# A fifth hidden tile by quarters in the second half of an FFN's output product

## The chip, the cores and the metric

The kernel runs on one core of a Trainium2 chip. The metric is the device time of one execution in microseconds (us). Each engine works through its own instructions in the order in which they were written into its queue: TensorE (PE; PEld is its loading of the stationary operand), VectorE (DVE), ScalarE (ACT), GpSimd (POOL), and SyncE (SP), which here issues the DMA transfers. Engines wait for one another by semaphores.

## The reference

One decoder layer on 512 tokens of width 1024: a first SwiGLU FFN, a token mixer, a second FFN, each between a norm before and a norm after, added to the residual stream.

```python
def swiglu_ffn(x, w_in, w_out):
    gate, up = jnp.split(x @ w_in, 2, axis=-1)
    return (jax.nn.silu(gate) * up) @ w_out

x = x + 0.5 * rms_norm(swiglu_ffn(rms_norm(x, norm_pre[l, 0]), ffn1_w_in[l], ffn1_w_out[l]),
                       norm_post[l, 0])
mixed = token_mixer(rms_norm(x, norm_pre[l, 1]), ...)
x = x + rms_norm(mixed, norm_post[l, 1])
x = x + 0.5 * rms_norm(swiglu_ffn(rms_norm(x, norm_pre[l, 2]), ffn2_w_in[l], ffn2_w_out[l]),
                       norm_post[l, 2])
```

The hidden width is 2816. The change lies in the product of the hidden values (512 x 2816) with `w_out` (2816 x 1024), which occurs twice, once in each FFN. The text calls the two FFNs the two layers.

## The kernel before

**Numbers in two parts.** TensorE multiplies in a rounded 32-bit format. To keep the precision, each operand is split into a high part (a cast on ScalarE) and a low part (the value less the high part, a subtraction on VectorE), and each product is made of three matmuls: high by high, high by low, low by high. A "split" below is such a pair of cast and subtraction. Every weight tile (L273 and L275 in `split`) and every hidden tile (`two_parts`, L812 and L813) is split once per use, 1024 columns wide on 128 partitions.

**The output product.** `ffn_out` (L858) works on the 1024 output columns in two halves. In each half it goes through 11 hidden tiles of 256 hidden columns, numbered 0 to 10, in the order `OUT` gives, and adds the products up in PSUM. The four blocks of 128 tokens and two quarters of the columns (256 each) are held in four accumulators `C[u][v]`: u is 0 for the even token blocks (0 and 2) and 1 for the odd ones. C takes four of the eight PSUM banks.

**Plain and quartered tiles.** A plain tile (`plain`, L886) takes 48 matmuls of 256 columns. A tile in `QUARTERED` is done by Strassen's method in Winograd's form: its hidden values and its weight are each cut into four quarters, sums of quarters are formed, and 7 products of 6 matmuls do the work of 8, 42 in all (`quartered`, L906, and `product`, L898). Four of the 7 products go into accumulators of their own, `M` (the other four PSUM banks), shared by all quartered tiles of a half; three go straight into C. After the last quartered tile of a half `common` (L922) copies one of the M to SBUF (ScalarE) and forms three more sums from M (four operations of VectorE, L863), and `add` (L932) adds the results to C, two operations for the odd blocks and two for the even ones (L863 as well: it is the line of the helper). The additions to the odd blocks need the copy and the second of the four operations, those to the even blocks the last two.

**What a quartered tile costs elsewhere.** Its weight is split twice: the three quarters used as they are (768 columns wide), then, after `sum_quarters` (L303, four VectorE operations of 256 columns, L306) has put the sums in the raw tile's place, all 1024 columns. Its hidden values need the parts of three quarters (`h_quarters`, L822), the sums (`h_sums`, L837, operations L844) and the parts of the sums (`s_tile`, L851). A tile that is quartered in both halves keeps the parts of its quarters and its sums (`stay`: the sums overwrite the hidden values) and makes only the parts of the sums anew in the second half.

**Places.** Split weights lie in four slots (`WBUF`): while one is multiplied, up to three are made ready, and a slot is free once TensorE has used its tile. Split hidden tiles and sums lie in three "s" places. The parts of quarters lie in the four idle places of the normed input (`PLACES`, `x_place`) or, for tiles 3 and 7, in the idle raw buffers of the weight loads (`RAW`, three of them; the name "once" in the profile). `LATER` puts hidden tiles 0 and 7 of the second half into those input places once the parts there are used. Tiles 9 and 10 keep their split form from the first half to the second. The "gpre" place holds a row of norm gains, and is read only while an input is normed.

**The end of the second half.** The last four tiles of `OUT[1]` (`LAST`) are plain and are taken together: for each token block i all four tiles are multiplied (`chunk`, L984; 48 matmuls per block, 12 per tile), so that the blocks are finished one after another and the norm after the FFN (`last`, L504) can begin. For block 0 the tiles go strictly one after the other. The odd additions (L982) stand ahead of the blocks, the even ones (L994) behind block 0. W0, W5, W7 and so on are the weights of hidden tiles 0, 5, 7.

**What sets the order.** The program is written as straight Python; a planner then fixes the order of each engine's instructions by a list of priorities (the order of writing) and its own estimate of when operands and places are free. So an instruction written later can stand ahead of an earlier one whose operand is not expected yet. On the chip this order is fixed. Loads of weights are issued on SP as soon as their raw buffer comes free in this plan.

Of the kernel before, what the change touches and what calls it, by code (L numbers as in the profile page):

```python
# [9 lines left out]
F32R = mybir.dt.float32r  # L10
AF = mybir.ActivationFunctionType
ALU = mybir.AluOpType
PSUM = bass.MemoryType.PSUM

P = 128
T = 512
D = 1024
# [5 lines left out]
RAW, WBUF, PAD, LATE, NEXT, FRONT, STEP = 3, 4, 128, 112, 64, 96, 16  # L23
PAIRS = NF // 2
# [54 lines left out]

QUARTERED = [(2, 3, 4, 6, 7, 8), (2, 4, 6, 8)]
OUT = [list(range(PAIRS)), [9, 2, 4, 10, 6, 8, 0, 1, 3, 5, 7]]
LAST = 4
PLACES, LATER = {2: 1, 4: 2, 6: 0, 8: 3}, {0: (1, 0), 7: (2, 3)}

AGAIN, ROWS = (9, 10), (18, 19, 20, 21)

# [27 lines left out]
class Layer:  # L116
# [705 lines left out]
    def h_quarters(self, k2, n=None):  # L822

        src = self.by_chunk(k2)
        parts = self.x_place(n) if n is not None else [
            self.wp.tile([P, D], F32R, tag="raw", bufs=RAW, name=self.nm("once"))[:, P - 2 * STEP :] for _ in range(2)
        ]
        parts = [v[:, : 3 * QUARTER].rearrange("p (k c t) -> p k c t", c=2, t=P) for v in parts]
        self.two_parts(*(v[:, 0] for v in parts), src[:, 0, 1])
        self.two_parts(*(v[:, 1:] for v in parts), src[:, 1])  # L830
        return [[None] + [v[:, j] for j in range(3)] for v in parts]
# [5 lines left out]
    def h_sums(self, k2, stay):  # L837

        a = self.by_chunk(k2)
        f = self.hf[:, 2 * k2 : 2 * k2 + 2, :]  # L840
        if not stay:
            f = self.sp.tile([P, 2, T], F32, tag="xn", bufs=1, name=self.nm("hsum"))
        v = f.rearrange("p k (c u t) -> p k u c t", u=2, t=P)
        tt = lambda out, x, y, op: self.nc.vector.tensor_tensor(out, x, y, op=op)  # L844
        tt(v[:, 0, 0], a[:, 0, 1], a[:, 0, 0], ALU.subtract)
        tt(v[:, 1, 0], v[:, 0, 0], a[:, 1, 0], ALU.add)
        for k in range(2):
            tt(v[:, k, 1], a[:, k, 1], v[:, 1, 0], ALU.subtract)
        return f

    def s_tile(self, f):  # L851
# [6 lines left out]
    def ffn_out(self, gpost_row, scale, after, trans, head):  # L858
# [10 lines left out]
        def more(n):  # L869
            while count[0] < min(n, len(seq)):  # L870
                half, k2 = seq[count[0]]
                count[0] += 1
                if k2 in QUARTERED[half]:
                    if k2 not in kept:
                        stay = k2 in QUARTERED[1]
                        kept[k2] = self.h_quarters(k2, PLACES.get(k2)), self.h_sums(k2, stay)
# [99 lines left out]
        for k2 in OUT[1][-LAST:]:  # L976
            ws.append(self.pull())
            more(n + 1)
            n += 1
        hs = [made.popleft()[0] for _ in range(LAST)]  # L980

# [836 lines left out]
```

## Time and profile before

| what | value |
|---|---|
| median of 3 runs | 937.53 us (937.38 to 937.99) |
| profiled execution, its own time | 939.23 us |
| its span | 937.5 us |
| granted TensorE clock | 0.999 |
| PE busy | 929.0 us (99%) |
| DVE busy | 772.9 us (82%) |
| ACT busy | 511.5 us (55%) |
| output product, layer 1 | from 223.99 to about 341.7 us |
| its second half, layer 1 | from about 282.5 us |

Times in rows count from the start of the span. In rows in order of time the columns are: start, length from the first start to the last end, engine, line, operation, output <- inputs with their shapes, and how many instructions are merged (x6); in brackets stands how long the engine was idle before it and what ended that. Operations of one engine overlap a little, so that the next starts before the last has ended. In rows of groups the columns are: what it is and how often, then busy time in us and the mean length of one in ns, then the idle time ahead of them.

### The profile page before, as it was taken

To read this page: it belongs to the slowest core of one execution; us is meant where nothing else is said; L and a number is where in the kernel's file an instruction comes from. 1 tells how busy PE (TensorE), PEld (TensorE's weight loads), DVE (VectorE), ACT (ScalarE), POOL (GpSimd) and SP (SyncE) were. 2 spreads that over 40 slices of the span, in tenths; PEclk is the share of its full clock that TensorE was granted. 3 is DMA by queue.
4 is the path that set the end of the run, shared out by engine and by line. 5 is a ranking of instruction groups with operands and counts; after the bars stand their busy time and mean duration, and the time that the engine had idled before them with its cause. 6 is when DMAs were issued, how large, how long until landed. Compare 5 with 4: busy or idle time off the path is not lost.

```text
span 937.5 us, 18056 instructions
## 1 busy us (share of the span) xinstructions
PE 929.0 (99%) x7471; PEld 894.4 (95%) x7471; DVE 772.9 (82%) x1044; ACT 511.5 (55%) x735; POOL 107.1 (11%) x172
## 2 busy tenths in 40 slices
PE   9999999999999999999999999999999999999997
PEld 7999999999999999998887887899999999999997
DVE  6899988889988876698846665799899889998884
ACT  7645455557456467956632445595354545655541
POOL 3530000000001045200011310314000000000101
PEclk9999999999999999999999999999999999999999
DMA  9252443332352034421312124352354435324212
GB/s 317 89 157 91 128 126 108 99 108 78 116 164 91 24 87 121 111 68 45 91 45 68 46 91 143 104 181 67 115 158 135 136 116 157 108 90 131 78 45 91
DMA packets 86956, 101.35 MB, mean 108 GB/s; under 512 B 4277, under 2 KB 66777, under 8 KB 86874
## 3 DMA queue, kind: packets, MB, share of 16 engines
q1 hardware_dynamic: 86586, 99.68, 34.8%
q8 instruction: 58, 0.95, 0.4%
q10 hardware_dynamic: 288, 0.52, 0.2%
q14 instruction: 24, 0.20, 0.1%
HBM read 98.10 MB, written 2.10 MB: 107 GB/s over the span
## 4 chain that ended last, share of the span: by engine, by line
PE 61%; ACT 1%; DMA 0%; DVE 0%; issue 0%; POOL 0%; DVEq 0%; POOLq 0%; ACTq 0%; SPq 0%
PE ps L603 22%; PE ps L893 7%; PE ps L533 6%; PE ps L901 5%; PE ps L179 5%; PE ps L181 4%; PE ps L180 4%; PE ps L1307 2%; PE ps L348 1%; PE ps L543 1%; PE ps L1482 0%; DMA raw<-in_ffn_w_in_dram 0%; PE ps L1393 0%; PE ps L1589 0%; PE ps L1562 0%; PE ps L1348 0%
## 5 line engine op out<-in xcount | busy, mean ns | idle before, releaser
L273 ACT CAST w<-raw 128x1024 fp32r<-128x1024 f32 (+1 forms) x238 | 244.4, 1034 | 233.1 <-PE ps L603 93.5
L275 DVE TENSOR_TENSOR w<-raw,w 128x1024 fp32r<-128x1024 f32 (+1 forms) x238 | 291.6, 1232 | 36.1 <-ACT w L273 35.3
L603 PE MATMUL ps<-xq,w 128*128 128x256 f32 x2016 | 237.4, 277 | 0.0
L603 PEld LDWEIGHTS ps<-xq,w 128*128 128x128 f32 x2016 | 233.2, 188 | 0.0
L603 PE MATMUL ps<-sq,w 128*128 128x256 f32 x1512 | 178.3, 277 | 0.3
L603 PEld LDWEIGHTS ps<-sq,w 128*128 128x128 f32 x1512 | 174.6, 188 | 0.9 <-ACT ps L654 0.9
L893 PE MATMUL ps<-w,hs 128*128 128x256 f32 x960 | 113.0, 276 | 0.0
L893 PEld LDWEIGHTS ps<-w,hs 128*128 128x128 f32 x960 | 110.7, 188 | 0.0
L289 DVE TENSOR_TENSOR raw<-raw,raw 128x1024 f32<-128x1024 f32 x72 | 89.9, 1251 | 8.1 <-DMA raw<-in_ffn_w_in_dram 6.6
L179 PE MATMUL ps<-w,xq 128*128 128x512 f32 x192 | 78.8, 411 | 0.1
L180 PE MATMUL ps<-w,xq 128*128 128x512 f32 x192 | 74.9, 391 | 0.1
L181 PE MATMUL ps<-w,xq 128*128 128x512 f32 x192 | 75.0, 392 | 0.0
L438 POOL TENSOR_SCALAR col<-col 128x1 f32<-128x1 f32 x24 | 9.0, 377 | 513.8 <-ACT junk L437 513.7
L533 PE MATMUL ps<-xq,w 128*128 128x256 f32 x480 | 58.1, 282 | 0.0
L901 PE MATMUL ps<-w,hs 128*128 128x256 f32 x480 | 57.7, 276 | 0.0
L533 PEld LDWEIGHTS ps<-xq,w 128*128 128x128 f32 x480 | 56.9, 189 | 0.5 <-issue 0.5
L901 PEld LDWEIGHTS ps<-w,hs 128*128 128x128 f32 x480 | 55.9, 188 | 0.0
L179 PEld LDWEIGHTS ps<-w,xq 128*128 128x128 f32 x192 | 36.1, 188 | 8.3 <-issue 0.9
L181 PEld LDWEIGHTS ps<-w,xq 128*128 128x128 f32 x192 | 36.0, 188 | 8.2 <-DVE xq L355 0.3
L812 ACT CAST hs<-hf 128x1024 fp32r<-128x1024 f32 x32 | 33.7, 1052 | 17.4 <-PE ps L901 10.7
L180 PEld LDWEIGHTS ps<-w,xq 128*128 128x128 f32 x192 | 36.2, 188 | 7.2 <-DVE w L281 0.5
L813 DVE TENSOR_TENSOR hs<-hf,hs 128x1024 fp32r<-128x1024 f32 x32 | 39.1, 1221 | 1.3 <-ACT hs L812 1.2
(258 smaller groups left out, 1140.4 us busy)
## 6 DMA issues: line engine op xcount, KB each, us to landing
raw<-in_ffn_w_in_dram SPq DMA_DIRECT2D x98, 512.0 KB, 3.7
raw<-in_ffn_w_out_dram SPq DMA_DIRECT2D x44, 512.0 KB, 4.2
raw<-in_w_mix_in_dram SPq DMA_DIRECT2D x28, 512.0 KB, 3.7
raw<-in_w_mix_out_dram SPq DMA_DIRECT2D x8, 512.0 KB, 3.9
out_dram<-xs SPq DMA_DIRECT2D x8, 256.0 KB, 2.0
xs<-in_x_dram SPq DMA_DIRECT2D x6, 256.0 KB, 4.1
gpost<-in_norm_post_dram SPq DMA_DIRECT2D x3, 512.0 KB, 3.5
gpre<-in_norm_pre_dram SPq DMA_DIRECT2D x2, 512.0 KB, 4.5
```

The source lines that it names most:

```text
L179: mm(ps, sh, mh, start=start, stop=False, **kw)
L180: mm(ps, sh, ml, start=False, stop=False, **kw)
L181: mm(ps, sl, mh, start=False, stop=stop, **kw)
L273: nc.scalar.copy(hi, raw)
L275: self.low = nc.vector.tensor_tensor(lo, raw, hi.bitcast(F32), op=ALU.subtract)
L289: (nc.vector if late else nc.gpsimd).tensor_tensor(o, o, c, op=ALU.add)
L533: mm(ps[:, u0:u1], w[:, a, k, :], self.xop(k, b, u0, u1), start=k + n + m == 0, stop=k == ND - 1 and n == 2, skip_group_check=True,)
L603: self.nc.tensor.matmul(ps[:, c], wb[b][:, k, v], left[d][:, k, :], start=first and a + n + k == 0, stop=n == 2 and k == KH - 1, skip_grou ...
L812: self.nc.scalar.copy(hi, src)
L813: self.nc.vector.tensor_tensor(lo, src, hi.bitcast(F32), op=ALU.subtract)
L893: mm(out, a[kk][:, i * P : (i + 1) * P], w[:, b, kk, QUARTER * v : QUARTER * (v + 1)], start=begin and c == kk == n == 0, stop=kk == 1 and ...
L901: mm(ps[:, QUARTER * c : QUARTER * (c + 1)], A[a][:, c], B[b], start=begin and c == n == 0, stop=n == 2, skip_group_check=True,)
```

## The change

In the second half of the columns tile 3 is quartered as well, so that the second half has five quartered tiles instead of four. The order of the second half becomes 9, 2, 4, 10, 3, 6, 8 and then the last four, 0, 1, 5, 7; before it was 9, 2, 4, 10, 6, 8, 0 and then 1, 3, 5, 7. There is no plain tile between the last quartered tile and the last four any more.

The parts of tile 3's quarters are kept from the first half to the second in the two raw buffers in which they were made, and its sums overwrite its hidden values. Tile 7, quartered only in the first half, puts its high parts into the third raw buffer and its low parts into the "gpre" place. Hidden tile 0 of the second half goes to an "s" place instead of the input places.

In `h_sums` the last two of four operations (256 columns each) become one of 512 columns, one operand of which is repeated over its two rows. This holds for every quartered tile.

```diff
-QUARTERED = [(2, 3, 4, 6, 7, 8), (2, 4, 6, 8)]
-OUT = [list(range(PAIRS)), [9, 2, 4, 10, 6, 8, 0, 1, 3, 5, 7]]
-LAST = 4
-PLACES, LATER = {2: 1, 4: 2, 6: 0, 8: 3}, {0: (1, 0), 7: (2, 3)}
+QUARTERED = [(2, 3, 4, 6, 7, 8), (2, 3, 4, 6, 8)]
+OUT = [list(range(PAIRS)), [9, 2, 4, 10, 3, 6, 8, 0, 1, 5, 7]]
+LAST, APART = 4, 7
+PLACES, LATER = {2: 1, 4: 2, 6: 0, 8: 3}, {7: (2, 3)}
...
     def h_quarters(self, k2, n=None):

         src = self.by_chunk(k2)
-        parts = self.x_place(n) if n is not None else [
-            self.wp.tile([P, D], F32R, tag="raw", bufs=RAW, name=self.nm("once"))[:, P - 2 * STEP :] for _ in range(2)
-        ]
+        once = lambda pool, tag, bufs, o: pool.tile([P, D], F32R, tag=tag, bufs=bufs, name=self.nm("once"))[:, o:]
+        if n is not None:
+            parts = self.x_place(n)
+        else:
+            places = [(self.wp, "raw", RAW, P - 2 * STEP), (self.cp, "gpre", 1, STEP // 2)]
+            parts = [once(*places[k2 == APART and m]) for m in range(2)]
...
         tt(v[:, 0, 0], a[:, 0, 1], a[:, 0, 0], ALU.subtract)
         tt(v[:, 1, 0], v[:, 0, 0], a[:, 1, 0], ALU.add)
-        for k in range(2):
-            tt(v[:, k, 1], a[:, k, 1], v[:, 1, 0], ALU.subtract)
+        tt(v[:, :, 1], a[:, :, 1], v[:, 1:2, 0].broadcast_to([P, 2, 2, P]), ALU.subtract)
         return f
```

## The prediction

> **What bounds the kernel now.** I read the page first: TensorE is busy nearly the whole span and holds most of the chain of work that ended last. Then the waits of TensorE: in 937 us it waits twice, once at the start. So TensorE sets the time. Matmuls taken out come back as time, unless something new makes TensorE wait.
>
> ```profile
> span 937.5 us, 18056 instructions
> PE 929.0 (99%) x7471; PEld 894.4 (95%) x7471; DVE 772.9 (82%) x1044; ACT 511.5 (55%) x735; POOL 107.1 (11%) x172
> PE ps L175 <- POOL ident masks.py:199: 1.5, 1, 1.5
> PE ps L603 <- ACT xq L368: 0.2, 1, 0.2
> ```
>
> Next the stretch that is changed, the second half of the columns. The busy time of each engine by stretch (length, then PE, PEld, DVE, ACT) shows the first layer's tiles 6 and 8, plain tile 0, and the first token block of the last four tiles; the last row is tile 0 in the second layer.
>
> ```profile
> 302.87:307.63 4.76, 4.76 (x44) 4.76 (x43) 3.53 (x5) 3.42 (x4) 0.00 (x0) 1.00 0.15 30
> 307.63:312.39 4.76, 4.76 (x44) 4.76 (x43) 4.76 (x5) 3.48 (x5) 0.00 (x0) 1.00 0.23 88
> 312.39:317.83 5.44, 5.44 (x50) 5.44 (x49) 5.44 (x8) 1.58 (x2) 0.00 (x0) 1.00 0.00 0
> 317.83:323.27 5.44, 5.44 (x50) 5.44 (x49) 3.34 (x5) 1.05 (x1) 0.00 (x0) 1.00 0.01 3
> 904.07:909.51 5.44, 5.44 (x50) 5.44 (x49) 5.44 (x8) 1.58 (x2) 0.00 (x0) 1.00 0.00 0
> ```
>
> TensorE is full in every row, but VectorE is full too from 307.63 to 317.83. A quartered tile lasts 4.76 us and a plain one 5.44. Both layers show the same stretch, 591.68 us apart. TensorE's own rows in order of time are plain tile 0 (48 matmuls in 5.44 us, 0.113 us each) and then the first token block, three tiles and the fourth:
>
> ```profile
> 312.39 5.60 PE L893 MATMUL ps<-w,xq 128*128 128x256 f32 x48
> 317.83 4.24 PE L893 MATMUL ps<-w,hs 128*128 128x256 f32 x36
> 321.91 1.52 PE L893 MATMUL ps<-w,xq 128*128 128x256 f32 x12
> ```
>
> What VectorE does beside it, also in order of time:
>
> ```profile
> 284.20 0.95 DVE L275 TENSOR_TENSOR w<-raw,w 128x768 fp32r<-128x768 f32 x1
> 285.06 2.38 DVE L475 TENSOR_TENSOR y<-ps,gpost 128x256 f32<-128x256 f32 x6
> ...
> 301.53 1.80 DVE L306 TENSOR_TENSOR raw<-raw 128x256 f32<-128x256 f32 x4
> 304.53 1.22 DVE L275 TENSOR_TENSOR w<-raw,w 128x1024 fp32r<-128x1024 f32 x1 [1.19 <-ACT w L273]
> 305.67 1.22 DVE L813 TENSOR_TENSOR hs<-hf,hs 128x1024 fp32r<-128x1024 f32 x1
> ...
> 312.48 0.68 DVE L863 TENSOR_TENSOR hf<-ps,hf 128x512 f32<-128x512 f32 x1
> 313.08 1.21 DVE L813 TENSOR_TENSOR xq<-hf,xq 128x1024 fp32r<-128x1024 f32 x1
> 314.22 0.68 DVE L863 TENSOR_TENSOR hf<-ps,hf 128x512 f32<-128x512 f32 x1
> 314.82 1.22 DVE L275 TENSOR_TENSOR w<-raw,w 128x1024 fp32r<-128x1024 f32 x1
> 315.95 0.68 DVE L863 TENSOR_TENSOR hf<-hf,ps 128x512 f32<-128x512 f32 x1
> 316.55 1.22 DVE L813 TENSOR_TENSOR hs<-hf,hs 128x1024 fp32r<-128x1024 f32 x1
> 317.69 0.68 DVE L863 TENSOR_TENSOR hf<-ps,hf 128x512 f32<-128x512 f32 x1
> 318.29 1.29 DVE L863 TENSOR_TENSOR ps<-ps,hf 128x512 f32<-128x512 f32 x2
> 319.48 1.22 DVE L275 TENSOR_TENSOR w<-raw,w 128x1024 fp32r<-128x1024 f32 x1
> 322.79 1.38 DVE L863 TENSOR_TENSOR ps<-ps,hf 128x512 f32<-128x512 f32 x2 [2.10 <-PE ps L893]
> ```
>
> From 304.53 to 320.62 there is no idle time. By start to start a 1024-wide operation takes 1.14 us (304.53 to 305.67), a 512-wide one 0.60 (312.48 to 313.08), the 768-wide split 0.86 (284.20 to 285.06). The four L863 to hf are the common sums. The pair at 318.29 adds two of them to the odd accumulators, and that at 322.79 the others to the even ones. The split at 319.48 is the last weight, W7.
>
> **The change part by part.** *Matmuls.* Tile 3 goes from 48 to 42 matmuls in each layer: 5.44 - 4.76 = 0.68 us, twice, so -1.36 us if nothing waits. This is all the change can save on TensorE.
>
> *Weight of tile 3.* Instead of one 1024-wide cast and subtraction it needs a 768-wide pair, four quarter sums and the 1024-wide pair. On VectorE that adds 0.86 + 1.80 = 2.66 us per layer, on ScalarE one 768-wide cast of 0.83 us, hidden since ScalarE is busy 3.4 to 3.5 of 4.76 us there. The hidden tile costs the same: it is split once in this half, from the sums instead of the values.
>
> ```profile
> L273 ACT CAST w<-raw 128x768 fp32r<-128x768 f32 x20 | 16.6, 831 | 0.2
> ```
>
> *The order.* Plain tile 0 moves behind the last quartered tile, into the last four, and tile 3 goes ahead of 6 and 8. So the four common sums and the splits for the last four tiles lose the 5.44 us of plain tile 0 as cover, and must run beside the last tiles themselves.
>
> *Where VectorE stands then.* After tile 10 ends at 302.87 come three quartered tiles, so the last four begin at 302.87 + 3 x 4.76 = 317.15, 0.68 earlier than now. VectorE's list from 304.53 on is the same eleven 1024-wide and six 512-wide operations, with a 768-wide split and four sums more: 16.09 + 2.66 = 18.75 us, so to 323.28 at the earliest. I add 0.6 of idle time: the split of W5 needs the place of tile 8's first weight half, free at 312.39 + 18 x 0.113 = 314.43, and a cast of 1.05 after it, so it starts near 315.75, while the seven 1024-wide operations ahead of it and the extra work end at 304.53 + 7 x 1.14 + 2.66 = 315.2. End: 323.9.
>
> *When TensorE needs it.* Of the first token block (48 matmuls, 12 per tile) the third tile's low half is needed at 317.15 + 26 x 0.113 = 320.1, W7's low half at 317.15 + 37 x 0.113 = 321.3, the low half of hidden tile 7 at 321.4, and the odd accumulators at 317.15 + 5.44 = 322.6. From 315.75 VectorE owes the W5 split, four common sums, hidden 5 and 7, W7 and the first odd addition: 4 x 1.14 + 5 x 0.60 = 7.6 us, to 323.3. If the two common sums for the even accumulators came last, it would be 322.1, in time. In the order that the rows above show, a common sum as soon as its operand is there and one split in each gap, I get W5 to 316.9, first sum 317.5, hidden 7 to 318.6, second sum 319.2, hidden 5 to 320.4 (0.4 late, with 0.1 for the signal: the cast at 318.03 below follows TensorE's last matmul of tile 0 by 0.20, the split at 304.53 its cast by 0.04), third sum 321.0, W7 to 322.1 (0.9 late, the 0.4 among it), fourth 322.7, first odd addition 323.3, when the delayed first block ends at 323.5: in time. Stall: 0.9 us per layer. The ends are 0 (best order) and W7 last of all, at 323.9 or, without my idle time, 323.3, against 321.3: 2.0 to 2.6, middle 2.3. I take 0.9, because its order is the one that the rows show. Before, W7 had 317.83 + 37 x 0.113 - 320.62 = 1.4 us of margin.
>
> *Queues.* ScalarE's casts stand in a fixed order, and one that must wait holds up those behind it:
>
> ```profile
> 303.44 1.05 ACT L273 CAST w<-raw 128x1024 fp32r<-128x1024 f32 x1 [2.45 <-DVE raw L306]
> 304.40 1.05 ACT L812 CAST hs<-hf 128x1024 fp32r<-128x1024 f32 x1
> 318.03 1.05 ACT L273 CAST w<-raw 128x1024 fp32r<-128x1024 f32 x1 [4.06 <-PE ps L893]
> ```
>
> The cast at 303.44 waited 2.45 us for sums; the cast behind it could have begun at 302.87, when tile 10's place came free. [...]
>
> *Places.* Tile 3's parts stay in two raw buffers until it is used again; tile 7's second part goes to the gain's place. So loads move on the SP queue:
>
> ```profile
> L152 SPq DMA_DIRECT2D gpre<-in_norm_pre_dram x2: 341/350/358, 28.3 to 350.6; - x2
> 248.68 0.46 SPq L236 DMA_DIRECT2D raw<-in_w_mix_in_dram  x1
> 269.13 0.46 SPq L236 DMA_DIRECT2D raw<-in_w_mix_in_dram  x1
> 272.82 0.44 SPq L236 DMA_DIRECT2D raw<-in_w_mix_in_dram  x1
> 329.37 1.43 DVE L465 SCALAR_TENSOR_TENSOR xn<-xs,col,gpre 128x512 f32<-128x512 f32 x2 [2.09 <-POOL col L442]
> 341.71 1.23 DVE L275 TENSOR_TENSOR w<-raw,w 128x1024 fp32r<-128x1024 f32 x1
> raw<-in_w_mix_in_dram SPq DMA_DIRECT2D x28, 512.0 KB, 3.7
> ```
>
> The next gain, now issued at 28.3, must wait until tile 7 has been used (about 267, behind which the load of 269.13 waits now); it is first read at 329.37. One mixer load waits as long, and two wait for tile 3's second use, 307.6; the first mixer weight is split at 341.71 and a load lands in 3.7 us. Over 25 us of cover, so 0; without it each late load would cost up to its 3.7. A weight load held up behind them is bounded the same way: W7's raw tile can be fetched from about 305.7, its cast is at 317.2. Below nothing: tile 7's second part no longer waits for tile 3's buffers, 1 us of VectorE earlier in the first half, where TensorE does not wait: 0.
>
> *Merged sums.* Two 256-wide operations become one of 512:
>
> ```profile
> 235.40 0.42 DVE L844 TENSOR_TENSOR hsum<-hf 128x256 f32<-128x256 f32 x1
> 235.73 0.42 DVE L306 TENSOR_TENSOR raw<-raw 128x256 f32<-128x256 f32 x1
> ```
>
> By start to start that is 2 x 0.33 against 0.60 us, 0.06 less for each of six tiles, all in the first half, where TensorE has no wait to lose: 0. Were the broadcast operand to double the operation, VectorE would lose 0.5 us per tile there.
>
> *Sum.* -1.36 + 2 x 0.9 = +0.4 us. Against the profiled execution's own 939.23 that is 939.7; the median of the runs is 1.70 below it, so 938.0.
>
> **The rivals.** *A, all is hidden:* the order happens to put the urgent splits first; 937.53 - 1.36 = 936.2. For it: VectorE's work up to the need just fits (322.1 against 322.6). Against: the order in the rows is not by urgency, and VectorE was already without idle time. *B, slower:* one wait takes the place of the saving, VectorE's W7 split coming last, behind the odd additions as at 319.48 now: TensorE then stops 2.3 us in each layer at the fourth tile, 937.53 - 1.36 + 4.6 = 940.8. It decides above 0.68 us of stall per layer. For it: W7 is last now. Against: it is so now because its cast starts only at 318.03; in the new order the cast is done at 318.7, before the third common sum. *C, the new order sets off a wait elsewhere* (a load held on SP, the slots of the mixer's weights shifted by one): bounded by one load, 3.7 us beside a saving of 1.36: 939.9. For it: TensorE's waits are so few that any new order can only add some. Against: the covers above are long.
>
> **How the numbers follow.** About 0.2%, 1.9 us, is what a measurement tells from no change. The forecast (stall 0.5 to 1.3 per layer, 937.2 to 938.8) has 0.39; A, with stalls under 0.5, 0.27; B, with stalls above 1.3, 0.24; C 0.10. Faster by 0.2% needs 935.65, beyond the matmuls' own saving: 0.03, from A with something I have not seen. Slower (over 939.4, stalls above 1.6 per layer): most of B and C, 0.28. The rest, 0.69, is within. The range runs from A to B: 936.1 to 940.9.
>
> **What would show it.** Right: TensorE's product rows have 42 matmuls for tile 3; the last four begin 0.68 us earlier in layer one; VectorE has no idle time until about 323.5; the waits of TensorE hold two new lines of about 1 us, on VectorE's splits at L275 or L813. Wrong: no such waits (A), a wait of over 2 us (B), waits in the mixer or at loads (C).

## The result, and the profile after

The changed kernel takes 944.72 us (median of 6 runs, 943.65 to 946.90), the kernel before in the same comparison 937.76 us (937.12 to 938.70). The ratio is 1.0078, with a 95% interval of 1.0068 to 1.0089: slower by 7.0 us, where 938.0 had been predicted. The profiled execution took 944.61 us.

The page of the changed kernel (span, then busy time and share of each engine):

```profile
span 942.6 us, 18034 instructions
PE 928.1 (98%) x7459; PEld 892.6 (95%) x7459; DVE 776.0 (82%) x1042; ACT 510.5 (54%) x737; POOL 105.3 (11%) x172
```

TensorE makes 12 matmuls less than before, as the change says, and VectorE works 3.1 us more. Now the waits of TensorE in the changed kernel (total, how often, longest; us), without the two that stood there before.

```profile
PE ps L895 <- DVE hs L813: 3.9, 2, 2.1
PE ps L543 <- ACT w L273: 1.7, 1, 1.7
...
PE ps L543 <- DVE w L275: 0.5, 1, 0.5
...
PE ps L903 <- DVE w L275: 0.2, 1, 0.2
```

Two new waits are for the low part of a hidden tile, one in each layer. The two at L543, the first matmuls of the mixer, come in the first layer alone. The small one at L903 is in the first half of layer 1, at the split that stands at 268.01 below. In order of time, TensorE in the last four tiles and at the start of the mixer (layer 1), then the last four tiles of layer 2:

```profile
317.59 4.92 PE L895 MATMUL ps<-w,hs 128*128 128x256 f32 x42
324.60 1.20 PE L895 MATMUL ps<-w,hs 128*128 128x256 f32 x8 [2.09 <-DVE hs L813]
...
345.46 4.81 PE L543 MATMUL ps<-xq,w 128*128 128x256 f32 x40 [1.68 <-ACT w L273]
...
910.87 4.92 PE L895 MATMUL ps<-w,hs 128*128 128x256 f32 x42
917.61 1.70 PE L895 MATMUL ps<-w,hs 128*128 128x256 f32 x8 [1.82 <-DVE hs L813]
919.11 2.66 PE L895 MATMUL ps<-w,xq 128*128 128x256 f32 x12
...
935.66 0.84 PE L895 MATMUL ps<-w,xq 128*128 128x256 f32 x6
```

The same places before:

```profile
341.74 6.13 PE L543 MATMUL ps<-xq,w 128*128 128x256 f32 x48
...
909.51 4.24 PE L893 MATMUL ps<-w,hs 128*128 128x256 f32 x36
...
930.59 0.84 PE L893 MATMUL ps<-w,xq 128*128 128x256 f32 x6
```

The first row of after holds 42 matmuls, not 28: tiles 0 and 1 (24), the high part of hidden tile 5 (4), and 14 that belong to block 1. The planner put those ahead, since it expected the low part of hidden tile 5 late. TensorE then still stops for 2.09 us.

Layer 1: the mixer begins at 345.46 and not at 341.74, 3.7 us later. Layer 2: from the start of the last four tiles to the end of the last matmul it was 930.59 + 0.84 - 909.51 = 21.92 us and is 935.66 + 0.84 - 910.87 = 25.63, so 3.7 more, less the 0.68 that tile 3 saves ahead of it: 3.0. The two make 6.7 of the 7.0 us. The other 0.3 lies outside the span: the profiled executions took 944.61 - 942.6 = 2.0 us more than their span after the change and 939.23 - 937.5 = 1.7 before. The spans differ by only 5.1, because the execution before was 1.7 us above its own median.

What made hidden tile 5 late is VectorE. Its rows in the changed kernel, layer 1:

```profile
268.01 2.36 DVE L275 TENSOR_TENSOR w<-raw,w 128x1024 fp32r<-128x1024 f32 x2 [1.19 <-ACT w L273]
...
296.60 1.80 DVE L306 TENSOR_TENSOR raw<-raw 128x256 f32<-128x256 f32 x4
...
305.71 1.22 DVE L275 TENSOR_TENSOR w<-raw,w 128x1024 fp32r<-128x1024 f32 x1 [1.20 <-ACT w L273]
...
312.99 2.36 DVE L275 TENSOR_TENSOR w<-raw,w 128x1024 fp32r<-128x1024 f32 x2 [1.19 <-ACT w L273]
...
319.87 1.21 DVE L813 TENSOR_TENSOR xq<-hf,xq 128x1024 fp32r<-128x1024 f32 x1
321.00 0.68 DVE L865 TENSOR_TENSOR hf<-ps,hf 128x512 f32<-128x512 f32 x1
321.60 1.21 DVE L275 TENSOR_TENSOR w<-raw,w 128x1024 fp32r<-128x1024 f32 x1
322.74 0.68 DVE L865 TENSOR_TENSOR hf<-hf,ps 128x512 f32<-128x512 f32 x1
323.33 1.22 DVE L813 TENSOR_TENSOR hs<-hf,hs 128x1024 fp32r<-128x1024 f32 x1
...
325.07 0.69 DVE L865 TENSOR_TENSOR ps<-ps,hf 128x512 f32<-128x512 f32 x1
326.52 1.38 DVE L865 TENSOR_TENSOR ps<-ps,hf 128x512 f32<-128x512 f32 x2 [0.77 <-PE ps L895]
```

The row at 323.33 is hidden tile 5, the last split of all, behind hidden 7 (319.87) and W7 (321.60). The list ends with the odd addition at 325.07, that is at 325.76; TensorE ends block 0, and the even additions start at 326.52. Two rows of before that answer to those at 268.01 and 296.60:

```profile
266.32 2.36 DVE L275 TENSOR_TENSOR w<-raw,w 128x1024 fp32r<-128x1024 f32 x2 [1.19 <-ACT w L273]
...
295.41 1.80 DVE L306 TENSOR_TENSOR raw<-raw 128x256 f32<-128x256 f32 x4
```

So VectorE was 1.69 us behind in the first half already, which cost TensorE the wait of 0.2 us there, and still 1.19 behind at 296.60. From there on the changed kernel has three chains of split, sums, cast and split (tiles 3, 6 and 8), with an idle time of 1.2 us in each, in which VectorE waits for ScalarE's cast of the sums; before there were two. The list ended at 320.62 before and ends at 325.76 now: 5.14 later, of which 1.19 was there at 296.60, 2.66 is tile 3's work and 1.2 its idle time.

In layer 1 the end of block 0 counts in full. The even additions start the norm behind the FFN, whose result the mixer needs. The mixer's first matmul waits for the cast of its weight, and that cast stands in ScalarE's queue right behind the norm's operations, without idle time and long after its load:

```profile
344.34 1.07 ACT L273 CAST w<-raw 128x1024 fp32r<-128x1024 f32 x1
```

From the start of the even additions to the mixer's first matmul it was 341.74 - 322.79 = 18.95 us before and is 345.46 - 326.52 = 18.94. Before, TensorE's own work ended at about the same time (341.6), so nothing showed; the start of the even additions has moved by 3.73 and the mixer by 3.72.

In layer 2 no mixer follows. There the wait of 1.82 counts, and with it something else. Stretches of the changed kernel (length, then PE, PEld, DVE, ACT, POOL; after them the granted clock):

```profile
324.60:326.87 2.27, 2.27 (x19) 2.27 (x20) 1.50 (x3) 0.00 (x0) 0.00 (x0) 1.00 0.04 7
917.60:919.10 1.50, 1.49 (x8) 1.49 (x9) 1.16 (x2) 0.00 (x0) 0.00 (x0) 0.67 0.00 0
919.10:921.60 2.50, 2.50 (x13) 2.50 (x13) 0.70 (x1) 0.18 (x1) 0.00 (x0) 0.52 0.00 0
```

The 20 matmuls behind the wait take 2.27 us in layer 1 and 4.00 us in layer 2, where the clock is down to 0.67 and 0.52. So 1.82 + 1.73 - 0.68 = 2.9 of the 3.0 us are named, in this execution.

### The profile page after: what moved, and what is told of

It reads as the page before. It is cut to its first block, busy times and chain, and to the rows that moved or that the text cites. A ratio compares the mean times of both kernels' runs of the same rounds, so it can differ in the third digit from the quotient of the medians.

```text
span 942.6 us, 18034 instructions
## 1 busy us (share of the span) xinstructions
PE 928.1 (98%) x7459; PEld 892.6 (95%) x7459; DVE 776.0 (82%) x1042; ACT 510.5 (54%) x737; POOL 105.3 (11%) x172
## 4 chain that ended last, share of the span: by engine, by line
PE 50%; DVE 9%; issue 2%; ACT 2%; POOL 0%; DVEq 0%; POOLq 0%; ACTq 0%
PE ps L603 19%; PE ps L533 6%; PE ps L179 5%; PE ps L181 5%; PE ps L180 5%; PE ps L895 3%; DVE w L275 3%; DVE hs L813 2%; PE ps L1309 2%; DVE raw L306 2%; ACT w L273 1%; PE ps L348 1%; PE ps L543 1%; DVE hf L847 0%; PE ps L1484 0%
## 5 line engine op out<-in xcount | busy, mean ns | idle before, releaser
L273 ACT CAST w<-raw 128x1024 fp32r<-128x1024 f32 (+1 forms) x240 | 245.6, 1032 | 246.8 <-PE ps L603 92.0
L895 PE MATMUL ps<-w,hs 128*128 128x256 f32 x960 | 114.1, 277 | 3.9 <-DVE hs L813 3.9
L895 PEld LDWEIGHTS ps<-w,hs 128*128 128x128 f32 x960 | 111.3, 188 | 4.3 <-DVE hs L813 4.3
L903 PE MATMUL ps<-w,hs 128*128 128x256 f32 x528 | 64.0, 277 | 0.2 <-DVE w L275 0.2
L903 PEld LDWEIGHTS ps<-w,hs 128*128 128x128 f32 x528 | 61.6, 188 | 0.5 <-DVE w L275 0.5
L813 DVE TENSOR_TENSOR hs<-hf,hs 128x1024 fp32r<-128x1024 f32 x36 | 43.8, 1217 | 0.0
L437 ACT ACTIVATE junk<-ps 128x256 f32<-128x256 f32 (+1 forms) x40 | 17.1, 428 | 46.6 <-DVE ps L865 23.0
```

What stands on the lines that cost most here:

```text
L273: nc.scalar.copy(hi, raw)
L813: self.nc.vector.tensor_tensor(lo, src, hi.bitcast(F32), op=ALU.subtract)
L895: mm(out, a[kk][:, i * P : (i + 1) * P], w[:, b, kk, QUARTER * v : QUARTER * (v + 1)], start=begin and c == kk == n == 0, stop=kk == 1 and ...
L903: mm(ps[:, QUARTER * c : QUARTER * (c + 1)], A[a][:, c], B[b], start=begin and c == n == 0, stop=n == 2, skip_group_check=True,)
```

## The experiments

The theory after these rows: VectorE's list has become the bound of this stretch. It ends too late because of the work of the fifth tile, because no plain tile is left behind the last quartered one as cover, or both. The rivals: the planned order of TensorE (14 matmuls of block 1 ahead), the place of one split in VectorE's order, the small parts of the change, and the clock. Each loss is counted against the runs of the kernel before that were made together with the experiment.

**The small parts alone.** The kernel before with the merged sums and tile 7's low parts in the gain's place.

```diff
-        for k in range(2):
-            tt(v[:, k, 1], a[:, k, 1], v[:, 1, 0], ALU.subtract)
+        tt(v[:, :, 1], a[:, :, 1], v[:, 1:2, 0].broadcast_to([P, 2, 2, P]), ALU.subtract)
...
+            places = [(self.wp, "raw", RAW, P - 2 * STEP), (self.cp, "gpre", 1, STEP // 2)]
```

> The kernel before, with two of the small parts of the change alone: the two subtractions of the sums merged into one, and the low quarters of tile 7 in the idle place of the gain row. Four tiles are quartered in the second half, in the order of before. If these parts cost nothing, as the prediction said, the time is that of before, 937.5 to 938.3. If they carry part of the loss of 7 (a load of the gain row that comes late, a longer subtraction in front of a split), it is above 939.

Measured: 937.59 us against 937.41, ratio 1.0005 (0.9996 to 1.0013). These parts cost no time. They do put VectorE behind in the first half. This row answers to those at 266.32 and 268.01:

```profile
267.41 2.36 DVE L275 TENSOR_TENSOR w<-raw,w 128x1024 fp32r<-128x1024 f32 x2 [1.19 <-ACT w L273]
```

That is 1.09 us later than before, but at 295.75, where 295.41 stood before, only 0.34 are left. So of the changed kernel's lag of 1.69 us these parts make 1.09, and little of what is left in the second half (1.19).

**Three last tiles, with tile 0 as cover again.**

```diff
-LAST, APART = 4, 7
+LAST, APART = 3, 7
```

> The changed kernel with one number altered: the last three tiles (1, 5, 7) are taken together instead of the last four, so that plain tile 0 stands again between the last quartered tile and the last ones. All five tiles stay quartered and all places stay as changed. Cover theory (the 5 us per layer are lost because no plain tile covers the splits that VectorE owes after the last quartered tile): no wait of TensorE on a split at the end of the second half, and 936.4 us (before less 1.36) if the norms can follow token blocks of 36 instead of 48 matmuls (4.1 us instead of 5.4); up to 939 if they cannot. Volume theory (VectorE's 2.66 us more per layer are simply too much wherever the plain tile stands): still waits of 1 to 2 us per layer, 941 to 944. Places theory (the buffers kept by tile 3 and the gain's place are what costs): no change from the changed kernel, 944.7.

Measured: 943.60 us against 938.21, ratio 1.0063 (1.0050 to 1.0076), so 5.4 us lost where it was 7.0; the two intervals overlap. The waits for hidden tile 5 are gone, but the even additions start at 326.62, as late as in the changed kernel. The mixer begins at 343.46, 1.7 us later than before, and TensorE waits 1.2 us twice for the norm's results (L348 for xn and hf). Taking the wait away at its place did not bring the end of block 0 forward. The waits in this trace are 3.6 us more than before; less the 1.36 us that the matmuls save, they name 2.2 of the 5.4.

**The order alone.** Tile 3 plain in the second half, everything else as changed. So VectorE has no work more than before, and TensorE saves nothing.

```diff
-QUARTERED = [(2, 3, 4, 6, 7, 8), (2, 3, 4, 6, 8)]
+QUARTERED = [(2, 3, 4, 6, 7, 8), (2, 4, 6, 8)]
```

> The order of the changed kernel (9, 2, 4, 10, 3, 6, 8 and then 0, 1, 5, 7), but tile 3 is plain in the second half, so VectorE has its old amount of work and TensorE its old 48 matmuls. Cover and volume together (my theory: both are needed): hidden tile 5's low part comes 2.7 us or more earlier than in the changed kernel (there at 324.55 against a need of about 320.5), so it is at most some tenths late, 937.8 to 939. Order alone: the lost cover is enough, waits as in the changed kernel, 943 or more. Places theory: tile 3 no longer keeps its buffers, so 937.8.

Measured: 940.54 us against 938.21, ratio 1.0027 (1.0016 to 1.0037). Rows of this kernel in order of time, one of ScalarE, one of TensorE and two of VectorE:

```profile
309.27 1.05 ACT L273 CAST w<-raw 128x1024 fp32r<-128x1024 f32 x1 [3.65 <-PE ps L895]
...
323.80 1.20 PE L895 MATMUL ps<-w,hs 128*128 128x256 f32 x8 [0.33 <-DVE hs L813]
...
322.52 1.22 DVE L813 TENSOR_TENSOR hs<-hf,hs 128x1024 fp32r<-128x1024 f32 x1
...
325.72 1.38 DVE L865 TENSOR_TENSOR ps<-ps,hf 128x512 f32<-128x512 f32 x2 [0.77 <-PE ps L895]
```

The same work ends 2.93 us later than before (325.72 against 322.79). With the plain tiles 10 and 3 ahead of the quartered ones, ScalarE's cast waits 3.65 us until TensorE gives a place free, VectorE waits behind it, and the work left over has no plain tile to run beside. So a third of the loss needs no fifth tile, and VectorE's amount of work is not the only cause: here it had idle time and could not use it.

**TensorE's order held.** The same kernel, and no matmul of block 1 may stand ahead of the last one of block 0.

```diff
+                with self.behind(*(mark if i == 1 else [])):
+                    z = plain(C, ws[n], hs[n], i, v, False)
+                if i == 0 and (v, n) == (1, LAST - 1):
+                    mark.append(z)
```

> The kernel of e2 (four quartered tiles, in the order that the change gives, tile 3 plain in the second half: 940.5 where before was 938.2), with TensorE's order set by hand: no matmul of block 1 may go ahead of the last one of block 0. Nothing is left out. If the 14 matmuls of block 1 that the planner put ahead make the additions of the even rows late, these start 1.6 us earlier in the first layer (14 times 0.113), and the time is 938.7 to 939.2. If those matmuls only fill a wait for the split of hidden tile 5, the wait grows from 0.33 to about 1.9, block 0 ends where it ended, and the time is 940.3 to 941.5.

Measured: 943.80 us against 937.44, ratio 1.0068 (1.0052 to 1.0085).

```profile
318.22 3.34 PE L895 MATMUL ps<-w,hs 128*128 128x256 f32 x28
323.46 1.20 PE L895 MATMUL ps<-w,hs 128*128 128x256 f32 x8 [1.90 <-DVE hs L813]
```

28 matmuls now stand ahead of the wait, and it grows from 0.33 to 1.90, by the 1.57 us that the 14 had filled. The planner's order is no cause of the loss; without it the loss would be larger. The time lies above both ranges that had been expected. A part of that goes with a lower clock (0.997 in the profiled execution, 0.999 with the order alone): behind the wait in layer 1 the next 12 matmuls take 2.60 us instead of 1.52.

**No sums for tile 3's weight.**

```diff
-        if it.sums:
+        if it.sums and it.key[2:] != (1, 3):
```

> The changed kernel without the four quarter sums of tile 3's weight in the second half (the second split then takes the unsummed quarters; the output is not the reference's). VectorE has 1.8 us less to do per layer at the same order. Cover and volume: hidden 5's low part comes 1.8 to 3 us earlier, so the first layer loses 0.7 to 1.9 instead of 3.7 us at that place and the second 0 to 1; 938 to 941. If the wait is not VectorE's amount of work but something behind the planned order alone (a place, a transfer): about 944.7 as before this edit.

Measured: 942.10 us against 938.21, ratio 1.0045 (1.0033 to 1.0058), so 3.9 of the 7.0 us are left, more than expected. The waits for hidden tile 5 are 1.02 us and about as much in layer 2, the granted clock of the execution stays at 0.998 and above. VectorE:

```profile
304.76 1.23 DVE L275 TENSOR_TENSOR w<-raw,w 128x1024 fp32r<-128x1024 f32 x1 [2.23 <-ACT w L273]
...
325.61 1.41 DVE L865 TENSOR_TENSOR ps<-ps,hf 128x512 f32<-128x512 f32 x2 [0.80 <-PE ps L895]
```

Of 1.80 us less work, 0.91 reaches the even additions (326.52 to 325.61). 1.03 turned into idle time ahead of the split at 304.76 (2.23 instead of 1.20). VectorE's sums for that tile were done at 302.53 (300.73 + 1.80). ScalarE's cast ahead of the split takes 1.05 us, so by my estimate it starts near 303.7, about 1.1 us later and right behind TensorE's plain tile 10, which ends at 303.59 (297.99 + 5.60). So here, by this estimate, the four places of the split weights hold VectorE up, and not its own work. No experiment gave them more room.

**Cover by plain tile 10.** First a version that also puts hidden tile 0 into the input places 1 and 0; there the last token blocks read other values in place of hidden tile 0, because the norm's transposes overwrite it, and TensorE waits 2.3 us for them (L355).

```diff
-OUT = [list(range(PAIRS)), [9, 2, 4, 10, 3, 6, 8, 0, 1, 5, 7]]
+OUT = [list(range(PAIRS)), [9, 2, 4, 3, 6, 8, 10, 0, 1, 5, 7]]
...
-PLACES, LATER = {2: 1, 4: 2, 6: 0, 8: 3}, {7: (2, 3)}
+PLACES, LATER = {2: 1, 4: 2, 6: 0, 8: 3}, {0: (1, 0), 7: (2, 3)}
```

> The changed kernel with the second half in the order 9, 2, 4, 3, 6, 8, 10 and then 0, 1, 5, 7: five quartered tiles in a row, and plain tile 10 between them and the last four; hidden tile 0 goes to the input places again. Cover theory: the last four find their splits done, 936.4 us; a small debt of VectorE within the five quartered tiles (4.9 to 5.1 us of work per 4.76 us) could cost up to 0.5 per layer. Volume theory: the debt of five quartered tiles in a row shows as waits within them, 940 or more. Places theory: 944.7.

Measured: 947.18 us against 938.21, ratio 1.0101 (1.0085 to 1.0116). With its own wait of 2.3 us and a clock of 0.64 behind it, it does not tell what cover is worth. The second version changes `OUT` alone:

> The changed kernel with the plain tile 10 moved behind the last quartered tile, in the place that plain tile 0 had before: the order of the second half is 9, 2, 4, 3, 6, 8, 10 and then 0, 1, 5, 7. All the work of the change stays, the four sums and the 768-wide split of tile 3 among it. If the loss comes from the lost cover, VectorE has 5.6 us of TensorE's work more to catch up in ahead of the last four, the waits for the split of hidden tile 5 go, the additions of the even rows start at 323 to 324 in the first layer, and the time is 936.4 to 938.5 (before, less two times 0.68, plus at most one small wait in each layer). If the loss comes from VectorE's volume (2.66 us more per layer, wherever the cover stands), a wait of 1.5 to 2 us stays in each layer, and the time is 941 or more.

Measured: 941.72 us against 937.41, ratio 1.0045 (1.0033 to 1.0058). Rows of TensorE, then one of VectorE:

```profile
306.19 2.27 PE L903 MATMUL ps<-w,hs 128*128 128x256 f32 x17 [0.74 <-DVE w L275]
...
322.79 1.42 PE L895 MATMUL ps<-w,hs 128*128 128x256 f32 x10 [0.25 <-DVE hs L813]
...
324.93 1.38 DVE L865 TENSOR_TENSOR ps<-ps,hf 128x512 f32<-128x512 f32 x2 [1.06 <-PE ps L895]
```

The time came out on the side of the rival, VectorE's volume, but not in its place: the wait for the split of hidden tile 5 is almost gone (0.25), and TensorE waits for the weights of the quartered tiles instead, which now follow one another. The even additions are still 2.1 us late. So cover gives back 2.7 of the 7.0 us, and 4.3 remain with VectorE's work and five quartered tiles in a row. Order alone costs 2.3, work with cover 4.3, both together 7.0. Not all of the 4.3 is named: the waits in this trace are 2.7 us more than before, and the matmuls save 1.36.

**The weight sums on GpSimd**, tile 3's alone in the changed kernel, the same with cover, and with cover for all five tiles of the second half.

```diff
-            self.sum_quarters(self.quarters(self.raw[it.key]))
+            self.sum_quarters(self.quarters(self.raw[it.key]), nc.gpsimd if it.key[2:] == (1, 3) else nc.vector)
```

> The changed kernel with the four sums of tile 3's weight in the second half made by GpSimd and no longer by VectorE. Nothing is left out. If VectorE's queue sets the loss, this takes the same 1.80 us per layer from it as leaving the sums out did (942.1), so the time is 941.8 to 942.8. If GpSimd's sums come too late for the split (its additions of 1024 columns took 2.64 us, so four of 256 may take 2.6 us and more) or hold VectorE up while they run, it is 944 or more.

> The kernel of the cover experiment (plain tile 10 behind the last quartered tile, 941.7), with tile 3's four weight sums on GpSimd. Nothing is left out. In e2 the order without cover cost 2.8 and in the cover experiment the work kept cost 4.3, so the two add up to the loss of 7. If the work is VectorE's, 1.80 us less of it per layer give back 2 to 2.6, as they did without cover (944.7 to 942.1), and the time is 939 to 939.8. If what is left of the loss lies in the split of 768 columns or in the three quartered tiles that follow one another, the time stays at 941 or more.

> The kernel of the cover experiment with the weight sums of all five quartered tiles of the second half on GpSimd, 9.0 us of VectorE's work per layer. Nothing is left out. If VectorE's queue sets the loss and GpSimd keeps up, the waits for weights ahead of the last four go and the saving of 0.68 per layer shows: 936 to 938, not slower than before. If GpSimd is the slower maker of the sums and TensorE comes to wait for them, or VectorE is held up by it, it is 940 or more.

Measured: 948.23 us (ratio 1.0115, 1.0099 to 1.0130), 946.57 (1.0095, 1.0080 to 1.0110) and 958.04 (1.0221, 1.0203 to 1.0238): each worse than with the sums on VectorE. Four sums took 3.17 us on GpSimd in the first and 4.1 us in the third kernel, against 1.80, and the cast and the split of the sums wait for them. In the first kernel VectorE, whose next operation is that split, stands idle for 4.38 us (300.95, "[4.38 <-ACT w L273]"), more than the 1.80 of the sums and the 1.17 of idle time that stood there. Here the longer chain cost more than the work that it took off the list: the first kernel loses 10.8 us (948.23 - 937.44) where it was 7.0.

**Two hidden tiles on GpSimd.** The subtractions of hidden tiles 1 and 5 have no such chain behind them.

```diff
-        self.nc.vector.tensor_tensor(lo, src, hi.bitcast(F32), op=ALU.subtract)
+        (engine or self.nc.vector).tensor_tensor(lo, src, hi.bitcast(F32), op=ALU.subtract)
```

> The changed kernel with the low halves of hidden tiles 1 and 5 of the last four made by GpSimd and no longer by VectorE. Nothing is left out. If only the length of VectorE's list counts, it ends 2 x 1.14 earlier, the additions of the even rows start at 324.3 to 324.7 in the first layer (326.52 before this edit), and the time is 940 to 942. If GpSimd's subtractions hold VectorE's up, as the additions of GpSimd in the mixers seem to do (a subtraction of 1024 columns on VectorE took 2.18 and 3.35 us beside them, otherwise 1.22), the list isn't shorter, and the time is 944 or more.

Measured: 948.06 us against 938.24, ratio 1.0103 (1.0089 to 1.0117). GpSimd's two rows and the two of VectorE beside them:

```profile
315.66 2.68 POOL L813 TENSOR_TENSOR hs<-hf,hs 128x1024 fp32r<-128x1024 f32 x1 [25.60 <-ACT hs L812]
318.98 2.69 POOL L813 TENSOR_TENSOR hs<-hf,hs 128x1024 fp32r<-128x1024 f32 x1 [0.64 <-ACT hs L812]
...
316.55 2.86 DVE L275 TENSOR_TENSOR w<-raw,w 128x1024 fp32r<-128x1024 f32 x1 [0.48 <-ACT w L273]
...
319.94 2.81 DVE L275 TENSOR_TENSOR w<-raw,w 128x1024 fp32r<-128x1024 f32 x1
```

Beside each GpSimd subtraction (2.68 and 2.69 us) one of VectorE takes 2.86 and 2.81 us instead of 1.22. The first ends at 319.41, 1.07 us after GpSimd's at 318.34, as if it had begun only then. So two operations of 1.14 us left the list, and the two beside GpSimd's became 3.2 us longer. In both pairs GpSimd's began first, 0.89 and 0.96 us ahead. What makes VectorE's longer there is not shown.

**The last two common sums later.** They are written behind block 0, so that hidden tile 5 goes ahead of them.

```diff
-            tt(x, q, M["p7"], ALU.subtract)
-            tt(y, M["p5"], x, ALU.subtract)
...
+                    rest(M, T)
                     add(C, T, 0)
```

> The changed kernel with the last two of the four common sums of the second half (c3 and c4) written behind the last matmul of block 0, and no longer behind the last quartered tile, so that VectorE makes the split of hidden tile 5 ahead of them. Nothing is left out. If the place of that split in VectorE's order makes the wait, the split ends about 1.1 us earlier in each layer (323.4 and not 324.55 in the first), the wait shrinks from 2.09 and 1.82 to about 1 and 0.7, with it the drop of the clock goes, and the time is 941.5 to 943. If only VectorE's volume counts, the additions of the even rows start as late as before the edit (326.5) in the first layer, since c3 and c4 come ahead of them anyway, and the time stays above 944.

Measured: 945.69 us against 937.41, ratio 1.0092 (1.0076 to 1.0107), no better than the changed kernel. The split of hidden tile 5 did end 0.6 us sooner, counted from the start of the last four tiles, but TensorE had 6 matmuls of block 1 less to run ahead (0.7 us), and the waits are 2.17 and 1.91 us. The even additions start at 326.65, right behind the delayed sums and without idle time of VectorE. So it came out on the side of VectorE's volume: this exchange within the list gives nothing back. The four runs lie apart: the one at 943.20 had a granted clock of 0.998 over the whole execution, the three at 945.55 to 946.67 had 0.995 and 0.996.

**The clock.** Filler matmuls in place of the wait in layer 2.

```diff
+                if self.second and i == 0 and (v, n) == (0, 2):
+                    self.spin(18)
```

> The changed kernel with 18 matmuls of 128 columns on an unused bank put in block 0 of the second layer, ahead of hidden tile 5's matmuls, so that TensorE isn't idle while it waits for the split. If the clock of 0.52 to 0.67 that was seen behind that gap comes from the gap, it doesn't show, the 20 matmuls behind it take 2.3 us and not 4.0, and the time is 1.7 lower: 942.8 to 943.2. If the slow stretch has another cause, or the extra matmuls cost as much as they save, it is 944.5 to 945.5.

Measured: 944.91 us against 937.41, ratio 1.0089 (1.0075 to 1.0104). Rows of TensorE, layer 2 and then layer 1:

```profile
917.31 4.18 PE L175 MATMUL ps<-ident 128*128 128x128 f32 x36
921.24 1.62 PE L895 MATMUL ps<-w,hs 128*128 128x256 f32 x12
...
325.02 2.02 PE L895 MATMUL ps<-w,hs 128*128 128x256 f32 x8 [2.12 <-DVE hs L813]
```

I had mis-sized the filler: 18 multiplications are 36 matmuls of 0.109 us, 3.9 us for a wait of 1.8, so it cost what it could have saved and the time decides nothing. The clock says more: behind the filler the matmuls run at 0.113 us and the granted clock is 1.00. In layer 1, where the wait of 2.12 us was left as it was, the clock fell in this execution (0.55 and 0.61 from 324.9 to 329.0), though it had not behind the 2.09 us of the changed kernel (1.00). So the drop is not tied to the place in layer 2, and it comes in some executions and not in others. By the granted clock of the whole execution it came in one of these five runs (0.996, the others 0.998 and more) and in four of the six of the changed kernel. That the filler prevents it is likely from this and not shown.

**One operation more.** The subtraction of hidden tile 5 in the last four made twice, in the changed kernel and in the kernel before.

```diff
         self.two_parts(hi, lo, src)
+        if again:
+            self.nc.vector.tensor_tensor(lo, src, hi.bitcast(F32), op=ALU.subtract)
```

> The changed kernel with the subtraction of hidden tile 5 in the last four made twice: one operation of 1024 columns, 1.14 us by start to start, more on VectorE's list in each layer. Nothing is left out. If VectorE's list sets the end of block 0, the additions of the even rows start 1.1 us later in the first layer (327.6), the wait in the second grows from 1.82 to about 2.95, and the time is 946.5 to 948. If something else sets it (the order of the matmuls, the places of the weights), it is under 945.5.

> The kernel before with the same subtraction made twice, 1.14 us more on VectorE's list in each layer. Nothing is left out. If VectorE had time to spare there before the change (the split of W7 ended at 320.62, and TensorE came to it at 322.0), nothing is lost: 937.3 to 938.2. If VectorE's list set the time before the change too, it is 939.5 or more.

Measured: the changed kernel goes to 951.27 us, 1.0138 (1.0122 to 1.0153) times the kernel before at 938.24. The kernel before goes to 937.96, 0.9996 (0.9987 to 1.0005). Changed kernel with the extra operation, TensorE and one row of VectorE:

```profile
326.89 1.20 PE L897 MATMUL ps<-w,hs 128*128 128x256 f32 x8 [2.00 <-DVE hs L821]
...
923.58 2.08 PE L897 MATMUL ps<-w,hs 128*128 128x256 f32 x8 [3.58 <-DVE hs L821]
925.46 2.76 PE L897 MATMUL ps<-w,xq 128*128 128x256 f32 x12
...
329.28 0.70 DVE L867 TENSOR_TENSOR ps<-ps,hf 128x512 f32<-128x512 f32 x1 [1.83 <-PE ps L897]
```

Kernel before with the extra operation, VectorE:

```profile
320.27 1.22 DVE L275 TENSOR_TENSOR w<-raw,w 128x1024 fp32r<-128x1024 f32 x1
...
323.05 1.38 DVE L865 TENSOR_TENSOR ps<-ps,hf 128x512 f32<-128x512 f32 x2 [0.95 <-PE ps L895]
```

This separates the two kernels. Before, VectorE had over 1.14 us to spare: the operation moved W7's split to 321.4, its idle time ahead of the even additions shrank from 2.10 to 0.95, and nothing was lost. Afterwards it has none: the loss grows from 7.0 to 13.0 us, so 2 x 1.14 us cost 6.1 us. That is more than the 2.3 of the work itself and above the range that had been expected: the wait in layer 2 grew by 1.76, and the clock fell behind the waits in both layers of the profiled execution (0.58 from 329 to 332, 0.50 from 922 to 925) and, by the granted clock of the whole execution (0.993 to 0.996), in all four runs.

None of these versions beats the kernel before.

## Why the prediction was wrong

*Matmuls, -0.68 per layer:* right in size. The last four tiles begin only 0.24 us earlier (317.59 against 317.83), since TensorE came 0.17 us later to the output product and lost the rest at the wait of 0.2 us in the first half. *Places, loads, merged sums, 0:* right as time for the parts that were tried alone; the buffers that tile 3 keeps were not tried alone. The sentence that 1 us of VectorE's work comes earlier in the first half holds, but it is no gain: the gap ahead of a split of sums that tile 7's low parts and the work around them used to fill stands empty, and VectorE is 1.69 us later at 268.01. I had looked for a wait of TensorE there, found none, and dropped it; VectorE carried 1.19 of it on into the second half.

*Where VectorE stands then:* this is the step that failed first. I began its list at 304.53 as if the change left that point alone, added 2.66 of work and 0.6 of idle time, and got 323.9. Measured is 325.76, with the same operations in the list. Missing are the 1.19 inherited from the first half and half of the 1.2 us of idle time that each chain of split, sums, cast and split brings. The row that shows the idle time, [1.19 <-ACT w L273] at 304.53, was in my own fence; I read it as the start of a full list and not as a cost that a further tile repeats.

*When TensorE needs it:* the walk put hidden tile 5 at 320.4 and W7 at 322.1 as the latest. Measured are 324.55 and 322.81: hidden 5 stood last, 4.2 us later than in the walk, 1.9 of it from the late list and the rest from the order. The wait is 2.09 and 1.82 us and not 0.9, and it would have been 3.7 and 3.4 without the 14 matmuls that the planner put in front; I had taken TensorE's order as fixed. The rival B, with one split coming last of all, was the right mechanism. It named W7, gave 2.3 us per layer, which the measured waits nearly meet, and still ended 4 us too low. That its 2.3 is near is luck, since it knew nothing of the 14 matmuls. Of rival C the sign is there, a wait in the mixer (1.68 us), but no load makes it.

*What the sum left out:* the end of block 0 itself. I said that the first odd addition comes in time and stopped there. The even additions start the norm, and from there to the mixer's first matmul it takes 18.95 us before and 18.94 after (18.92 with the order alone, 18.93 with cover by tile 10; 16.84 with only three last tiles), and before the change the end of that fell on the end of TensorE's own work (341.74 against about 341.6). So in layer 1 TensorE had no slack for a later start, and the 3.73 us counted in full, the saved matmuls and the 14 moved ones included. By my sum each layer would lose 0.9 - 0.68 = 0.2 us; it lost 3.7 and 3.0. The last term is the clock: 1.73 us behind a wait of 1.82 in layer 2, in the profiled execution.

*The order in ScalarE's and VectorE's queues:* I took a strict order of both queues as a reason for the walk. The rows of the changed kernel agree with it: the cast of hidden tile 5 (317.13, 1.05 us) was done at 318.18, and VectorE came to its split at 323.33, behind splits that were less urgent. That the order is strict everywhere was my assumption.

*What the experiments settle:* the new order costs 2.3 us without any new work, the new work 4.3 us with cover. VectorE's list has no room left (one operation more costs more than its length), where before it had more than 1.14 us. Moving one split or holding TensorE's order does not help, and bringing tile 0 back as cover with only three last tiles leaves 5.4 us; each leaves the list as long as it is. What stays open is how the 7.0 us divide between the 1.19 us of the first half and the second half's own idle time: the first was read from the traces and not taken away by itself. Open too is what more than four places for split weights would give: with less work on VectorE than in the changed kernel, ScalarE's cast waits for a place (about 1.1 us behind VectorE's sums in the kernel without tile 3's, by my estimate; 3.65 us with the order alone).

## What to carry to other kernels

Where an engine is full in a stage, price an added step from the whole chain that it repeats, its idle time included, and take the start of the list from the stage before, because a lag that costs nothing there is carried on. Test the margin directly: make one operation twice; if the time doesn't move, there is room, and if it does, look for work to take off the list or for work of the other engine to run beside it. And ask of each block that comes later which fixed chain it starts: its delay counts in full if that chain ends together with the work that was to hide it.

## What the runs showed of the hardware

The granted clock fell behind waits of 1.8 to 3.6 us in some executions and stayed in others. In the kernels whose longest wait of TensorE, by the one trace of each, was 1.67 us or less (the kernel before, and those with the parts alone, three last tiles, the order alone, no sums, cover by tile 10, cover with tile 3's sums on GpSimd, and the doubled operation in the kernel before) the granted clock of the whole execution was 0.998 or more in every run. In the kernels with a wait of 1.8 us or more it was 0.993 to 0.997 in some of the runs or in all: four of six in the changed kernel, three of four with the later common sums, all four with the doubled operation. Where it fell in a trace, it was 0.67 and 0.52 behind 1.82 us (changed kernel, 917.60 to 921.60), 0.55 and 0.61 behind 2.12 (the filler's kernel, layer 1, 324.9 to 329.0), 0.64 behind 2.32 (first cover version, 342.3 to 347.0), and 0.58 and 0.50 behind 2.00 and 3.58 (the doubled operation). It stayed at 1.00 behind 2.09 us in layer 1 of the changed kernel, in the same execution in which it fell behind 1.82, and behind 2.17 and 1.91 with the later common sums. So the length of the wait alone doesn't decide it, and what else does is not shown.

Two subtractions of VectorE took 2.86 and 2.81 us beside GpSimd's of 2.68 and 2.69, otherwise 1.22, and ended 1.07 and 1.08 us after GpSimd's.

The spacing of matmuls of 256 columns is not one number at a granted clock of 1.00. It is 0.113 us in most stretches (5.44 / 48 in the plain tiles of the kernel before). In others it is 0.118 (34.09 / 288), without a wait in them. The same 288 matmuls of the mixer, first in the kernel before, then in the changed kernel:

```profile
355.11 34.09 PE L533 MATMUL ps<-xq,w 128*128 128x256 f32 x288
...
359.08 32.80 PE L533 MATMUL ps<-xq,w 128*128 128x256 f32 x288
```

The 1.29 us between them are most of the 1.7 us by which the profiled execution before lies above its median. Such stretches come at other places in other executions: in the first cover version from 320.24 to 336.50 (16.26 / 138). Their cause is not known.
